# The first weight tile of two up projections in three products of 256 columns

## The chip, the cores and the metric

The kernel runs on one core of a Trainium2 chip. The metric is the device time of one execution in microseconds (us); the number that counts is the median of several executions. TensorE (PE in the profile) multiplies; it has a queue of its own for the loads of its stationary operand (PEld). VectorE (DVE), ScalarE (ACT) and GpSimd (POOL) do the rest, and SyncE (SP) issues the weight transfers.

## The reference: what is computed

One decoder layer on 256 tokens of width 2048 in float32: a norm, a combined input projection, attention in eight heads beside a pooling mixer, an output projection into the residual stream, and then a gated MLP of inner width 5632 with a short convolution over time:

```python
def conv_ffn(h, w_up, conv_w, conv_b, w_down):
    u = h @ w_up
    ...
    for i in range(CONV_WIDTH):
        y = y + conv_w[i] * u_pad[:, i:i + S]
    gate, val = jnp.split(y, 2, axis=-1)
    return (jax.nn.silu(gate) * val) @ w_down

...
    x = x + conv_ffn(rms_norm(x, ffn_norm_g[l]), w_up[l], conv_w[l], conv_b[l], w_down[l])
```

The change lies in `h @ w_up`.

## The kernel before

**High and low parts.** Every float32 operand is split into a rounded part and a remainder: `wh` and `wl` of the weights, index 0 and 1 of the third axis of the activations. A product in float32 is then the sum of three: high by high, high by low, low by high. The rounded copy of a weight chunk is made on ACT (`high`, L150), its remainder on DVE (`low`, L156).

**Chunks.** All weights come as a row of chunks of 128 x 2048, loaded by SP into four `raw` buffers in turn, and each chunk is used in two halves, the steps `u = 2 * c` and `u = 2 * c + 1`. The steps stand in one list, and the loop at the end of `layer` runs through it, so that the order of the products on TensorE is the order of that list.

**Up projections.** A block of 256 output features takes four steps (`feat_block`). Its accumulator `ps_feat` is a pair of PSUM banks from the pool tag `acc`, one bank for each `m`, 512 columns wide: the left 256 columns for the high part of the activations (`S` is 256), the right 256 for everything that is to be added to it. `feat_half` calls `feat_mm` for each of the two banks, and `feat_mm` goes over four weight tiles of 128 x 128. For each it issues two products: `wh` against high and low part side by side, 512 columns (L235), and `wl` against the high part, 256 columns, added to the right half (L237). A weight tile is thus a pair of products, 512 and 256 columns, each with a load of its own of the stationary operand, which here is the weights. The activations are `xh` in the input projection, `cat` in the output projection and `x2h` in the MLP.

**The other forms.** The token-major input projections (`tok_half`, L228; `val_half`, L209 and L218) and the down projection (`product`, L822, called by `seven_products` and `eight_products`) keep the activations stationary and move the weights, in products of 512 columns throughout. The pooling mixer (`feat_sum`, L244) takes three products of 256 columns for each weight tile: `wh` by the high part, `wh` by the low part, `wl` by the high part. Attention (L456, L492, L494) has products of 128 and 256 columns.

**The MLP in thirds.** The inner width is done in three parts (`THIRDS`) of 8, 8 and 6 blocks of 256: the up projections of a part for gate and value, 16, 16 and 12 blocks of 32 weight tiles, and then its down projection into 2048 columns. So there are two places where an up projection follows a down projection: chunk 97, step 194, and chunk 145, step 290. The first third's up projection, from step 98 on, follows the output projection, which is of the same form as itself. Before the down projection's last accumulators are free again, DVE has to add them to the residual (`done`, L900).

Of the kernel before, what the change touches and what calls it, by code (L numbers as in the profile page):

```python
# [31 lines left out]
S = 256  # L32
# [11 lines left out]
HALF = CH // 2  # L44
AHEAD = 5
FROM = 52
RAWS = 4

C_FFN, C_PS, C_QG, C_KG, C_CW, C_CB = 0, 16, 24, 25, 26, 26 + 3 * 2 * NF
# [33 lines left out]
def layer(ctx: ExitStack, tc: tile.TileContext, xT, wts, par, rel_d, ident_d, icnt_d, out):  # L83
    nc = tc.nc
# [15 lines left out]
    def small(name):  # L100
        return sm.tile([P, 512], F32, name=name, tag="small")
# [9 lines left out]
    def load(c, lo=0, n=CH, queue=None):  # L111

        if c not in raws:
            raws[c] = wpool.tile([P, CH], F32, name="raw", tag="raw", bufs=RAWS)
        s = slice(lo, lo + n)
# [24 lines left out]
    def split(c):  # L140
        split_piece(c, 0, CH)
        release(c)
# [3 lines left out]
    def high(c):  # L146

        wparts[c] = w, = (high_tile(c),)
        for lo, n in PIECES.get(kinds[c], ((0, CH),)):
            nc.scalar.activation(w[:, lo:lo + n], raws[c][:, lo:lo + n], AF.Copy)  # L150

    def low(c):

        wh, wl, r = *wparts[c], low_tile(c), raws[c]
        for lo, n in PIECES.get(kinds[c], ((0, CH),)):
            nc.vector.tensor_tensor(wl[:, lo:lo + n], r[:, lo:lo + n], wh[:, lo:lo + n].bitcast(F32), op=OP.subtract)  # L156
        wparts[c] = wh, wl
        if kinds[c] == "seven":
            wparts[c] += right_sums(r)
        release(c)  # L160
# [22 lines left out]
    def half(u):  # L183

        parts = wparts[u // 2] if u % 2 == 0 else wparts.pop(u // 2)
        return tuple(w[:, (u % 2) * HALF:(u % 2 + 1) * HALF] for w in parts)

    def release(c):

        raws.pop(c)  # L190
        c += RAWS
        if c < KT // 2:
# [39 lines left out]
    def feat_mm(ps, wh, wl, act, ks, first, last):  # L232

        for n, (ws, k) in enumerate(ks):
            nc.tensor.matmul(ps, wh[:, ws], act[:, k, :, :],  # L235
                             start=(first and n == 0), stop=False, skip_group_check=True)
            nc.tensor.matmul(ps[:, S:], wl[:, ws], act[:, k, 0, :], start=False,  # L237
                             stop=(last and n == len(ks) - 1), skip_group_check=True)

# [7 lines left out]
    def feat_half(u, act, k0, ps, first, last, mm=feat_mm):  # L247
        wh, wl = half(u)
        for m in range(2):
            mm(ps[m], wh, wl, act,  # L250
               [(slice(k * 256 + m * P, k * 256 + (m + 1) * P), k0 + k) for k in range(4)],
               first, last)


    xh = keep.tile([P, KT, 2, S], F32R, name="xh", tag="h")
# [29 lines left out]
    ps = small("ps_start")  # L285
# [291 lines left out]
    def feat_block(act, ks, post, final=False):  # L577
        box, runs = {}, []
        for i, k0 in enumerate(ks):
            def run(u, i=i, k0=k0):  # L580
                if i == 0:
                    box["acc"] = None if final else acc("ps_feat")
                    box["ps"] = [small("ps_feat")[:, :S] if final else box["acc"][:, m, :] for m in range(2)]
                feat_half(u, act(), k0, box["ps"], i == 0, i == len(ks) - 1, feat_sum if final else feat_mm)
                if i == len(ks) - 1:
                    post(box["ps"] if final else box["acc"])
            runs.append([run])
        return runs
# [46 lines left out]
    for b in range(2):  # L635
# [6 lines left out]
        for j in range(4):  # L642
            h = 4 * b + j
            u, ul, uo = ((32, 35, 40), (40, 44, 48), (48, 52, 55), (55, 59, 63))[h // 2]
# [286 lines left out]
    n = len(steps)  # L931
    assert n == 2 * wts.shape[0], (n, wts.shape)
    for u in range(n):
# [4 lines left out]
        elif u >= 4 and u % 2 == 0:  # L938
            c, now[0] = u // 2 + 2, u
            if c < FROM:  # L940
                split(c)
            if c >= FROM - 1 and c + 1 < wts.shape[0]:
                high(c + 1)
            if FROM <= c < wts.shape[0]:
                splits.append(lambda c=c: low(c))
# [83 lines left out]
```

## Time and profile before

| | us |
|---|---|
| median of 3 executions | 1010.86 |
| lowest, highest | 1009.64, 1010.89 |
| the profiled execution's own time | 1010.22 |
| its span in the trace | 1008.5 |
| mean granted clock of TensorE in it | 0.999 |

A row of a group of instructions reads: line, engine, operation, output and inputs by the program's names, tile sizes, count, then the busy time of the group, the mean duration of one in ns and the idle time ahead of it. A row of the timeline begins with the start and the duration in us. Products overlap in the trace: the next begins while the one before still has its end to write, so a duration is longer than the distance from one start to the next. Busy time counts each moment once. The distance between starts is the time that a product costs in a stream.

### The profile page before, as it was taken

How to read it: one execution, taken by the hardware profiler on the slowest of the kernel's cores; microseconds unless marked ns; L12 is line 12 of the kernel's file. 1: busy time of each engine (PE TensorE's matmuls, PEld its weight loads, DVE VectorE, ACT ScalarE, POOL GpSimd, SP SyncE). 2: the span in 40 equal slices, each digit the busy share in tenths (PEclk: the TensorE clock that was granted, in tenths of full speed). 3: DMA queues.
4: the chain of work that ended last, by engine and by line, in shares of the span. 5: the costliest groups of instructions: out<-in, count | busy, mean ns of one | idle time of the engine just before them, and what ended most of it. 6: DMA issues, size and time to landing. Idle time of an engine off the chain costs nothing.

```text
span 1008.5 us, 13232 instructions
## 1 busy us (share of the span) xinstructions
PE 1002.6 (99%) x5304; PEld 860.8 (85%) x5304; DVE 802.1 (80%) x943; ACT 529.4 (52%) x560; POOL 61.3 (6%) x119
## 2 busy tenths in 40 slices
PE   9999999999999999999999999999999999999998
PEld 8888888888888888888888888888888888888886
DVE  6776859857679878789996777778899867877996
ACT  6554545555556655556453545455564444555641
POOL 0302232200003300000000000000000000000000
PEclk9999999999999999999999999999999999999999
DMA  9958785665558855554556455554554665555361
GB/s 349 316 209 280 253 260 194 212 251 198 218 178 266 301 187 203 202 175 169 207 209 251 167 173 203 182 194 168 183 211 153 245 209 172 204 174 202 127 232 58
DMA packets 36156, 210.34 MB, mean 209 GB/s; under 512 B 5288, under 2 KB 7720, under 8 KB 13184
## 3 DMA queue, kind: packets, MB, share of 16 engines
q1 hardware_dynamic: 31408, 197.58, 55.7%
q0 software_dynamic: 4688, 11.94, 4.2%
q8 instruction: 41, 0.67, 0.3%
q14 instruction: 19, 0.16, 0.0%
HBM read 201.23 MB, written 8.26 MB: 208 GB/s over the span
## 4 chain that ended last, share of the span: by engine, by line
PE 91%; issue 4%; DMA 3%; DVE 1%; POOL 1%; SPq 0%; ACT 0%; POOLq 0%; DVEq 0%
PE ps_feat L235 41%; PE ps_down L822 23%; PE ps_feat L237 20%; PE ps_val L218 4%; PE ps_tok L228 2%; DMA qT<-q1d 1%; DMA eT<-e3d 1%; DMA q0d<-q0x 1%; PE ps_pool L244 1%; DMA eT<-e0d 1%; DMA raw<-in_wts 0%; DVE wl L125 0%; POOL qT L435 0%; DMA e0d<-e0x 0%; PE ps_s L456 0%
## 5 line engine op out<-in xcount | busy, mean ns | idle before, releaser
L235 PE MATMUL ps_feat<-x2h,wh 128*128 128x512 f32 x1408 | 490.8, 394 | 0.0
L237 PE MATMUL ps_feat<-x2h,wl 128*128 128x256 f32 x1408 | 391.3, 278 | 0.0
L235 PEld LDWEIGHTS ps_feat<-x2h,wh 128*128 128x128 f32 x1408 | 263.7, 187 | 63.2
L156 DVE TENSOR_TENSOR wl<-raw,wh 128x2048 fp32r<-128x2048 f32 (+2 forms) x145 | 286.1, 1990 | 3.3 <-issue 3.3
L237 PEld LDWEIGHTS ps_feat<-x2h,wl 128*128 128x128 f32 x1408 | 264.3, 188 | 0.1
L150 ACT ACTIVATE wh<-raw 128x2048 fp32r<-128x2048 f32 (+2 forms) x145 | 241.3, 1676 | 40.9 <-PE ps_down L822 30.8
L822 PE MATMUL ps_down<-wh,hid 128*128 128x512 f32 x512 | 163.2, 389 | 0.0
L125 DVE TENSOR_TENSOR wl<-raw,wh 128x2048 fp32r<-128x2048 f32 (+3 forms) x60 | 119.6, 2000 | 49.7 <-ACT wh L124 41.2
L505 DVE TENSOR_TENSOR fs<-ps_feat,fs 128x512 f32<-128x512 f32 x52 | 35.9, 691 | 107.6 <-ACT fs L504 107.6
L822 PEld LDWEIGHTS ps_down<-wh,hid 128*128 128x128 f32 x512 | 96.1, 188 | 19.9
L124 ACT ACTIVATE wh<-raw 128x2048 fp32r<-128x2048 f32 (+3 forms) x60 | 99.9, 1681 | 10.9 <-DMA raw<-in_wts 7.7
L822 PE MATMUL ps_down<-wl,hid 128*128 128x512 f32 x256 | 99.6, 389 | 0.0
L235 PE MATMUL ps_feat<-cat,wh 128*128 128x512 f32 x256 | 87.3, 389 | 0.0
L504 ACT ACTIVATE fs<-ps_feat 128x512 f32<-128x512 f32 x52 | 31.1, 597 | 94.0 <-PE ps_feat L237 92.1
L228 PE MATMUL ps_tok<-wh,xh 128*128 128x512 f32 x256 | 80.1, 391 | 0.0
L237 PE MATMUL ps_feat<-cat,wl 128*128 128x256 f32 x256 | 70.7, 276 | 0.0
L178 ACT ACTIVATE th<-raw 128x1024 fp32r<-128x1024 f32 x32 | 34.0, 1063 | 50.9 <-DVE raw L167 45.7
L235 PEld LDWEIGHTS ps_feat<-cat,wh 128*128 128x128 f32 x256 | 48.1, 188 | 10.0
L228 PEld LDWEIGHTS ps_tok<-wh,xh 128*128 128x128 f32 x256 | 48.1, 188 | 10.0
L822 PEld LDWEIGHTS ps_down<-wl,hid 128*128 128x128 f32 x256 | 48.0, 188 | 9.9
L797 ACT ACTIVATE hid<-y 128x512 fp32r<-128x512 f32 x22 | 13.9, 633 | 76.8 <-DVE y L796 76.8
L228 PE MATMUL ps_tok<-wl,xh 128*128 128x512 f32 x128 | 49.8, 389 | 0.0
(194 smaller groups left out, 1075.7 us busy)
## 6 DMA issues: line engine op xcount, KB each, us to landing
raw<-in_wts SPq DMA_DIRECT2D x178, 1024.0 KB, 4.8
raw<-in_wts SPq DMA_DIRECT2D x4, 512.0 KB, 7.2
x2d<-x2x POOLq DMA_DIRECT2D x4, 512.0 KB, 6.5
x<-x2d POOLq DMA_DIRECT2D x32, 64.0 KB, 5.8
xboth<-in_xT SPq DMA_DIRECT2D x6, 256.0 KB, 10.0
out<-x SPq DMA_DIRECT2D x3, 512.0 KB, 3.5
x2f<-in_xT SPq DMA_DIRECT2D x1, 1024.0 KB, 8.6
x2f<-in_xT SPq DMA_DIRECT2D x1, 768.0 KB, 6.6
```

The lines of the kernel that those rows point to most:

```text
L124: nc.scalar.activation(wh, w, AF.Copy)
L125: nc.vector.tensor_tensor(wl, w, wh.bitcast(F32), op=OP.subtract)
L150: nc.scalar.activation(w[:, lo:lo + n], raws[c][:, lo:lo + n], AF.Copy)
L156: nc.vector.tensor_tensor(wl[:, lo:lo + n], r[:, lo:lo + n], wh[:, lo:lo + n].bitcast(F32), op=OP.subtract)
L178: nc.scalar.activation(part(t[0]), part(r), AF.Copy)
L218: nc.tensor.matmul(ps[b][:, t, :], xh[:, k, a, ts], w[:, ws], start=False, stop=(k == KT - 1 and n == 2), skip_group_check=True)
L228: nc.tensor.matmul(ps[:, t, :], act[:, k0 + k, a, ts], w[:, ws], start=(first and k == 0 and n == 0), stop=(last and k == 1 and n == 2))
L235: nc.tensor.matmul(ps, wh[:, ws], act[:, k, :, :], start=(first and n == 0), stop=False, skip_group_check=True)
L237: nc.tensor.matmul(ps[:, S:], wl[:, ws], act[:, k, 0, :], start=False, stop=(last and n == len(ks) - 1), skip_group_check=True)
L504: nc.scalar.activation(dst, ps[:, :, S:], AF.Copy)
L505: nc.vector.tensor_tensor(dst, ps[:, :, :S], dst, op=OP.add)
L822: nc.tensor.matmul(ps, a, w, start=(first and n == 0), stop=(last and n == 2), skip_group_check=True)
```

## The change

The constant `AFTER_DOWN` names the two chunks. In their first half, for the first bank (`m == 0`) and the first of the four weight tiles, the product of 512 columns is made as two of 256: one for the high part of the activations into the left half of the bank, one for the low part into the right half. The first of them carries the start flag. The third product, `wl` by the high part, is as before. All else is as before: 2 of the 896 weight tiles of those two up projections are touched.

```diff
+AFTER_DOWN = (97, 145)
...
     def feat_mm(ps, wh, wl, act, ks, first, last):
 
         for n, (ws, k) in enumerate(ks):
-            nc.tensor.matmul(ps, wh[:, ws], act[:, k, :, :],
-                             start=(first and n == 0), stop=False, skip_group_check=True)
+            if first == "apart" and n == 0:
+                for a in range(2):
+                    nc.tensor.matmul(ps[:, a * S:(a + 1) * S], wh[:, ws], act[:, k, a, :],
+                                     start=(a == 0), stop=False, skip_group_check=True)
+            else:
+                nc.tensor.matmul(ps, wh[:, ws], act[:, k, :, :],
+                                 start=(bool(first) and n == 0), stop=False, skip_group_check=True)
             nc.tensor.matmul(ps[:, S:], wl[:, ws], act[:, k, 0, :], start=False,
                              stop=(last and n == len(ks) - 1), skip_group_check=True)
...
             mm(ps[m], wh, wl, act,
                [(slice(k * 256 + m * P, k * 256 + (m + 1) * P), k0 + k) for k in range(4)],
-               first, last)
+               "apart" if first and m == 0 and u // 2 in AFTER_DOWN else first, last)
```

TensorE's queue at the first place, step 194, where the down projection of the first third ends. `ps_down` are its accumulators, `hid` its stationary activations; the numbers tell buffers apart. Before:

```order
L822 MATMUL ps_down_4292<-wl_4460,hid_2672 128x512
L822 MATMUL ps_down_4292<-wh_4428,hid_2672 128x512
L235 MATMUL ps_feat_4563<-x2h_1931,wh_4458 128x512 [waits DVE_49,Activation_49]
L237 MATMUL ps_feat_4563<-x2h_1931,wl_4497 128x256
L235 MATMUL ps_feat_4563<-x2h_1931,wh_4458 128x512
L237 MATMUL ps_feat_4563<-x2h_1931,wl_4497 128x256
```

And with the change (the products' lines are now L828, L238 for the two halves, L241 for 512 columns and L243 for `wl`):

```order
L828 MATMUL ps_down_4292<-wl_4460,hid_2672 128x512
L828 MATMUL ps_down_4292<-wh_4428,hid_2672 128x512
L238 MATMUL ps_feat_4563<-x2h_1931,wh_4458 128x256 [waits DVE_49,Activation_49]
L238 MATMUL ps_feat_4563<-x2h_1931,wh_4458 128x256
L243 MATMUL ps_feat_4563<-x2h_1931,wl_4497 128x256
L241 MATMUL ps_feat_4563<-x2h_1931,wh_4458 128x512
L243 MATMUL ps_feat_4563<-x2h_1931,wl_4497 128x256
```

One row has become two, with the wait on the first of them; nothing else has moved. The second place, step 290, where the down projection of the second third ends, on the same engine, before:

```order
L822 MATMUL ps_down_6329<-wh_6465,hid_4733 128x512
L235 MATMUL ps_feat_6600<-x2h_1931,wh_6495 128x512 [waits DVE_49,Activation_49]
L237 MATMUL ps_feat_6600<-x2h_1931,wl_6534 128x256
L235 MATMUL ps_feat_6600<-x2h_1931,wh_6495 128x512
L237 MATMUL ps_feat_6600<-x2h_1931,wl_6534 128x256
```

And with the change:

```order
L828 MATMUL ps_down_6330<-wh_6466,hid_4734 128x512
L238 MATMUL ps_feat_6601<-x2h_1931,wh_6496 128x256 [waits DVE_49,Activation_49]
L238 MATMUL ps_feat_6601<-x2h_1931,wh_6496 128x256
L243 MATMUL ps_feat_6601<-x2h_1931,wl_6535 128x256
L241 MATMUL ps_feat_6601<-x2h_1931,wh_6496 128x512
L243 MATMUL ps_feat_6601<-x2h_1931,wl_6535 128x256
```

Here too one row is two, and the rest stands as it was (the buffers' numbers are one higher, for the product that came in earlier). On DVE, ACT, POOL and SP the instructions and their order are the same in both kernels.

## The prediction

> **What bounds the kernel now.** I read the page first, its busy times and the chain that ended last:
>
> ```profile
> span 1008.5 us, 13232 instructions
> PE 1002.6 (99%) x5304; PEld 860.8 (85%) x5304; DVE 802.1 (80%) x943; ACT 529.4 (52%) x560; POOL 61.3 (6%) x119
> ...
> PE ps_feat L235 41%; PE ps_down L822 23%; PE ps_feat L237 20%; PE ps_val L218 4%; PE ps_tok L228 2%; DMA qT<-q1d 1%; DMA eT<-e3d 1%; DMA q0d<-q0x 1%; PE ps_pool L244 1%; DMA eT<-e0d 1%; DMA raw<-in_wts 0%; DVE wl L125 0%; POOL qT L435 0%; DMA e0d<-e0x 0%; PE ps_s L456 0%
> ```
>
> TensorE has work all the time, and the chain is made of its products. So there is hardly a wait to remove, and the time changes only if products themselves follow each other at another distance. That is the second thing to read. The busy times by stage, for two stretches of 160 us, the first within the up projection of the first third, the second within that of the second third, and one within that of the last third (columns: PE, PEld, DVE, ACT, POOL, clock, DMA share, GB/s):
>
> ```profile
> 285.00:445.00 160.00, 160.00 (x943) 141.54 (x942) 132.54 (x164) 90.84 (x97) 20.66 (x38) 1.00 0.67 222
> 542.20:702.20 160.00, 160.00 (x908) 138.20 (x907) 117.82 (x137) 83.20 (x85) 0.00 (x0) 1.00 0.55 191
> 806.10:941.70 135.60, 135.60 (x770) 117.16 (x769) 101.59 (x118) 70.47 (x73) 0.00 (x0) 1.00 0.54 187
> ```
>
> In the same 160 us, TensorE is busy throughout in both stretches and its granted clock is 1.00 in both, yet it makes 943 products in the first and 908 in the second. The two up projections are the same code with the same tile sizes. The groups by shape, over the whole of each up projection, give the size of it:
>
> ```profile
> L235 PE MATMUL ps_feat<-x2h,wh 128*128 128x512 f32 x512 | 174.1, 389 | 0.0
> ...
> L235 PE MATMUL ps_feat<-x2h,wh 128*128 128x512 f32 x512 | 180.9, 397 | 0.0
> ...
> L235 PE MATMUL ps_feat<-x2h,wh 128*128 128x512 f32 x384 | 135.7, 397 | 0.0
> ```
>
> A product of 512 columns lasts past the start of the next of its kind, so the busy time of this group is the stage without a gap, and divided by the count it is the distance from one pair (512 and 256 columns) to the next: 174.1 / 512 = 340.0 ns in the first third, 180.9 / 512 = 353.3 ns in the second, 135.7 / 384 = 353.4 ns in the last. I call these the short and the long pace. The difference is 13.3 ns a pair.
>
> **What separates the two.** Since clock, code and shapes are equal, I looked at how each stretch of pairs begins. The timeline of TensorE at the place of the change, out of the down projection:
>
> ```profile
> 541.88 0.39 PE L822 MATMUL ps_down<-wh,hid 128*128 128x512 f32 x1
> 542.11 0.39 PE L235 MATMUL ps_feat<-x2h,wh 128*128 128x512 f32 x1
> 542.34 0.28 PE L237 MATMUL ps_feat<-x2h,wl 128*128 128x256 f32 x1
> 542.46 0.40 PE L235 MATMUL ps_feat<-x2h,wh 128*128 128x512 f32 x1
> 542.69 0.28 PE L237 MATMUL ps_feat<-x2h,wl 128*128 128x256 f32 x1
> 542.81 0.40 PE L235 MATMUL ps_feat<-x2h,wh 128*128 128x512 f32 x1
> ...
> 805.98 0.39 PE L235 MATMUL ps_feat<-x2h,wh 128*128 128x512 f32 x1
> 806.21 0.28 PE L237 MATMUL ps_feat<-x2h,wl 128*128 128x256 f32 x1
> 806.33 0.40 PE L235 MATMUL ps_feat<-x2h,wh 128*128 128x512 f32 x1
> ...
> 806.68 0.40 PE L235 MATMUL ps_feat<-x2h,wh 128*128 128x512 f32 x1
> ```
>
> No product waits here: the first pair follows the last product of the down projection after 0.23 us, as those follow each other. The pairs are at the long pace from the first on (542.11, 542.46, 542.81), and both places look the same to the hundredth. A third stretch comes directly out of products of 512 columns, in the input projection behind L228, and it has the long duration of 397 ns as well:
>
> ```profile
> L235 PE MATMUL ps_feat<-xh,wh 128*128 128x512 f32 x8 | 2.9, 397 | 0.0
> ```
>
> Those 8 pairs end where attention's small products cut in. Behind these, and behind the pooling mixer's products of 256 columns, the groups are others:
>
> ```profile
> L235 PE MATMUL ps_feat<-xh,wh 128*128 128x512 f32 x52 | 17.7, 389 | 0.0
> ...
> L235 PE MATMUL ps_feat<-xh,wh 128*128 128x512 f32 x61 | 20.8, 389 | 0.0
> ...
> L235 PE MATMUL ps_feat<-cat,wh 128*128 128x512 f32 x230 | 78.3, 389 | 0.0
> ```
>
> The first two of these groups stand behind attention's products, from 148.9 and from 170.5 us on, and have 17.7 / 52 = 340 and 20.8 / 61 = 341 ns a pair; the third stands behind the mixer's products, from 207.1 us on, with 78.3 / 230 = 340. How TensorE comes into the last of them:
>
> ```profile
> 206.01 0.28 PE L244 MATMUL ps_pool<-cat,wl 128*128 128x256 f32 x1
> 206.13 0.39 PE L235 MATMUL ps_feat<-cat,wh 128*128 128x512 f32 x1
> ...
> 206.48 0.40 PE L235 MATMUL ps_feat<-cat,wh 128*128 128x512 f32 x1
> ...
> 206.84 0.39 PE L235 MATMUL ps_feat<-cat,wh 128*128 128x512 f32 x1
> ...
> 207.18 0.39 PE L235 MATMUL ps_feat<-cat,wh 128*128 128x512 f32 x1
> ```
>
> The pairs from 206.13 on are 0.35, 0.36 and 0.34 us apart: they begin at about the long pace and find the short one within three pairs. That stretch, once in, runs to the end of the first third's up projection without leaving it. So there are two steady paces; a stretch of pairs falls into one of them in its first microsecond and stays there for hundreds of pairs, and which one depends on what TensorE did just before. In this trace all entries from a product of 512 columns into a pair go to the long pace (three), all entries by way of shorter products to the short one: the three of the quoted groups, and two shorter stretches between them that do the same.
>
> **The change part by part.** It replaces the first pair at both places by three products of 256 columns, in the order `wh`, `wh`, `wl` in which the mixer makes its own.
>
> *The products themselves.* The chain of work has the mixer's 24 products in a row as one piece, start and length in us:
>
> ```profile
> 197.90 2.82 PE ps_pool L244 x24
> ```
>
> A product of 256 columns in a row of its like costs 2.82 / 24 = 0.118 us. Three of them are 0.354 us in place of the first pair's 0.35 (542.11 to 542.46): nothing that the rows resolve, at most 0.01 us at each of the two places. Their additional load of the stationary operand is in that distance already, since each of the mixer's products has its own. The wait on ACT and DVE moves to the first of the three and nothing was waited for there; behind it the queue is as before. Bounds: nothing below, and 0.24 us above, if each of the two additional products came on top with its whole 0.118 us.
>
> *The pace behind them.* This is the term that matters and that the trace doesn't show for this sequence: no stretch in it comes out of 512 columns by way of only three of 256. The nearest rows bound it: 353.3 ns a pair if nothing changes, 340.0 ns if the alternation locks into the short pace. I take the short pace, because the last three products ahead of the pair at 206.13 are the same three in the same order with the same weight layout, and that entry goes to the short pace in three pairs. Then the second third gains 180.9 − 174.1 = 6.8 us, and the last 135.7 − 384 x 0.3400 = 5.1 us. Together 11.9 us. Each entry costs some of it: the three pairs from 206.13 to 207.18 took 1.05 us, 0.03 over 3 x 0.340, so with the three products 0.04 us a place, 0.1 for both.
>
> *What could take it back.* A quicker TensorE asks for weights sooner. The first third shows that the rest keeps up: at 340 ns it had DVE at 132.54 of 160 us with more beside it than the later thirds have (the residual's turn on POOL), ACT at 90.84 and the DMA engines at 0.67, and PE 160.00 of 160. So no new bound is late next. The down projections keep their own pace.
>
> The sum: 1010.22 for the profiled execution, − 11.9 + 0.1 = 998.4 us. That execution is 0.64 below the median of the runs, 1010.86, from which it would be 999.1; I predict 998.8.
>
> **A rule that speaks against it.** The trace's rows above say that one and the same pair of products costs 340.0 or 353.3 ns at the same granted clock. The Trainium skill, in "TensorE: Matmul & The Clock Gate", section "Back-to-back issue gap", gives the distance of a warm product as its columns over 2.4 GHz and about 2.5 ns, with no memory of what came before. By that rule a pair of 512 and 256 columns is an estimated 325 ns everywhere, the change adds two products and no columns, an estimated 5 ns in all, and the time stays. The trace disagrees with it twice, by the level and by having two of them, so I give this outcome the chance of the second rival only.
>
> **The rivals.**
>
> 1. *One place only.* The first sequence locks into the short pace and the other doesn't, or the pace is lost on the way. For it: the trace shows single entries, not why. Against it: the entries at 542.11 and 805.98 are alike in every start, and no long stretch changes its pace. With the second third alone 1010.22 − 6.8 = 1003.4, with the last alone 1005.1; 0.6 more from the median.
> 2. *Nothing.* Three products of 256 columns are too few, or what decides was set in the down projection; the pairs go on at 353. For it: at the long pace too each 512 follows a 256, and that doesn't free it; and the mixer's entry followed 24 short products, not three. The price is that of the two additional products, under 0.24 us: 1010.2, from the median 1010.9.
> 3. *A worse pace, slower.* The alternation locks beyond 353 ns. For it: pairs of 0.36 us are seen while a stretch settles (206.48 to 206.84). Against it: no stretch stays there. If all 896 pairs ran at 0.36 us, it would be 896 x 6.7 ns = 6.0 us more, 1016.2; it decides the sign measurably from 2.0 / 896 = 2.2 ns over the long pace.
>
> **How the numbers follow.** Both places at the short pace 0.70, one place 0.07, nothing 0.20, a worse pace 0.03. A measurement of this kernel tells a change of about 0.2%, or 2 us, from none. So faster 0.77, same 0.21, slower 0.02 (a third of the worst case stays within 2 us). The forecast's own range is 997.6 to 1000.2: 998.4 and 999.1 with the spread of the three runs. It holds 0.70, so the range has to reach to the case of no change, up to 1011.2.
>
> **What would show each step.** In the changed kernel's trace the groups of L241, 512 columns, should have about 174 us for 511 pairs in the second third and 130.5 for 383 in the last, mean durations of 389 and not 397 ns, and TensorE's products in 160 us behind the first place should be some 943 and not 908. The timeline should show three starts about 0.12 us apart, then two or three pairs of 0.35 and from there 0.34. The last third should start 6.8 us sooner. If the pairs behind the three products stay 0.35 apart, the step on the entry is wrong and the time stays near 1010.5; if they reach 0.34 but TensorE then shows idle time behind DVE or a weight transfer, the step on the cover is wrong.

## The result, and the profile after

The changed kernel takes 998.22 us, median of 4 runs (997.55 to 999.07), against 1010.8 before: a ratio of 0.9879, with a 95% interval of 0.9867 to 0.989. The profiled execution took 999.07 us, its span 997.3.

The page's first lines for the changed kernel, to be read beside those of before: TensorE is busy for 99% as it was. It has two products more and is busy 11.9 us less, in a span that is 11.2 us shorter.

```profile
span 997.3 us, 13236 instructions
## 1 busy us (share of the span) xinstructions
PE 990.7 (99%) x5306; PEld 856.8 (86%) x5306; DVE 802.1 (80%) x943; ACT 528.9 (53%) x560; POOL 61.4 (6%) x119
```

The busy times of the changed kernel by stretch, the same columns and, for the first two, the same stretches as before:

```profile
285.00:445.00 160.00, 160.00 (x943) 141.91 (x942) 131.87 (x164) 90.25 (x95) 20.73 (x38) 1.00 0.67 222
542.20:702.20 160.00, 160.00 (x943) 141.68 (x942) 123.65 (x144) 84.71 (x88) 0.00 (x0) 1.00 0.57 195
799.50:930.00 130.50, 130.50 (x769) 115.42 (x768) 101.14 (x117) 69.70 (x72) 0.00 (x0) 1.00 0.56 195
```

160 us of the second third now hold 943 products, as many as in the first third, where they held 908. The granted clock is 1.00 throughout, so the clock is no part of it. The groups of the changed kernel's wide products by stage: the second third, the last third, and a stretch of the input projection from 148.9 to 166.2 us:

```profile
L241 PE MATMUL ps_feat<-x2h,wh 128*128 128x512 f32 x511 | 173.8, 389 | 0.0
...
L241 PE MATMUL ps_feat<-x2h,wh 128*128 128x512 f32 x383 | 130.3, 389 | 0.0
...
L241 PE MATMUL ps_feat<-xh,wh 128*128 128x512 f32 x51 | 18.1, 397 | 0.0
```

173.8 / 511 and 130.3 / 383 are both 340 ns a pair: the short pace, at both places. The third row is one that the prediction did not expect. The same stretch in the same 17.3 us had 52 pairs at a mean duration of 389 ns before, and has 51 at 397 now: the long pace, in a part of the program that the change does not touch.

How TensorE of the changed kernel comes out of the down projection, start and duration in us:

```profile
542.55 0.39 PE L828 MATMUL ps_down<-wh,hid 128*128 128x512 f32 x1
542.78 0.40 PE L238 MATMUL ps_feat<-x2h,wh 128*128 128x256 f32 x2
543.01 0.28 PE L243 MATMUL ps_feat<-x2h,wl 128*128 128x256 f32 x1
543.13 0.39 PE L241 MATMUL ps_feat<-x2h,wh 128*128 128x512 f32 x1
...
543.48 0.40 PE L241 MATMUL ps_feat<-x2h,wh 128*128 128x512 f32 x1
...
543.84 0.39 PE L241 MATMUL ps_feat<-x2h,wh 128*128 128x512 f32 x1
...
799.88 0.40 PE L238 MATMUL ps_feat<-x2h,wh 128*128 128x256 f32 x2
```

Three products in 0.35 us, pairs 0.35 and 0.36 apart, then the short pace.

The difference of the two profiled executions closes from these starts. The first place is reached at 542.78 in place of 542.11, 0.67 us later; that is the stretch at the long pace above, some 55 pairs x 13.3 ns = 0.7. So the last third starts 6.1 us sooner, at 799.88, and not the 6.8 of the gain alone. From the first place to the second it takes 257.10 in place of 263.87 us, 6.77 less; from the second to the end of the span 197.4 in place of 202.5, 5.1 less. 0.67 − 6.77 − 5.1 = − 11.2, and the spans differ by 1008.5 − 997.3 = 11.2.

### The profile page after: what moved, and what is told of

It reads as the page before. It is cut to its first block, busy times and chain, and to the rows that moved or that the text cites. A ratio compares the mean times of both kernels' runs of the same rounds, so it can differ in the third digit from the quotient of the medians.

```text
span 997.3 us, 13236 instructions
## 1 busy us (share of the span) xinstructions
PE 990.7 (99%) x5306; PEld 856.8 (86%) x5306; DVE 802.1 (80%) x943; ACT 528.9 (53%) x560; POOL 61.4 (6%) x119
## 4 chain that ended last, share of the span: by engine, by line
PE 91%; issue 4%; DMA 3%; DVE 1%; POOL 1%; SPq 0%; ACT 0%; POOLq 0%; DVEq 0%
PE ps_feat L241 41%; PE ps_down L828 23%; PE ps_feat L243 20%; PE ps_val L219 4%; PE ps_tok L229 2%; DMA qT<-q1d 1%; DMA eT<-e3d 1%; DMA q0d<-q0x 1%; PE ps_pool L250 1%; DMA eT<-e0d 1%; DMA raw<-in_wts 0%; DVE wl L126 0%; POOL qT L441 0%; DMA e0d<-e0x 0%; PE ps_s L462 0%
## 5 line engine op out<-in xcount | busy, mean ns | idle before, releaser
L241 PE MATMUL ps_feat<-x2h,wh 128*128 128x512 f32 x1406 | 478.2, 389 | 0.0
L243 PE MATMUL ps_feat<-x2h,wl 128*128 128x256 f32 x1408 | 388.6, 276 | 0.0
L241 PEld LDWEIGHTS ps_feat<-x2h,wh 128*128 128x128 f32 x1406 | 263.9, 188 | 54.6
L243 PEld LDWEIGHTS ps_feat<-x2h,wl 128*128 128x128 f32 x1408 | 264.3, 188 | 0.0
L828 PE MATMUL ps_down<-wh,hid 128*128 128x512 f32 x512 | 163.3, 389 | 0.0
L828 PEld LDWEIGHTS ps_down<-wh,hid 128*128 128x128 f32 x512 | 96.1, 188 | 20.0
L828 PE MATMUL ps_down<-wl,hid 128*128 128x512 f32 x256 | 99.6, 389 | 0.0
L241 PE MATMUL ps_feat<-cat,wh 128*128 128x512 f32 x256 | 87.3, 389 | 0.0
L243 PE MATMUL ps_feat<-cat,wl 128*128 128x256 f32 x256 | 70.7, 276 | 0.0
L828 PEld LDWEIGHTS ps_down<-wl,hid 128*128 128x128 f32 x256 | 48.1, 188 | 9.9
L241 PEld LDWEIGHTS ps_feat<-cat,wh 128*128 128x128 f32 x256 | 48.1, 188 | 9.8
```

What stands on the lines that cost most here:

```text
L241: nc.tensor.matmul(ps, wh[:, ws], act[:, k, :, :], start=(bool(first) and n == 0), stop=False, skip_group_check=True)
L828: nc.tensor.matmul(ps, a, w, start=(first and n == 0), stop=(last and n == 2), skip_group_check=True)
```

## The experiments

What was to be told apart: does each entry set the pace of its own stretch; does it take three products, halves, or anything short; is it the entry alone or can a stretch be freed later; does a row of 512-column products lead to the long pace by itself; and what makes two paces out of one sequence of products.

### One place alone

```diff
-AFTER_DOWN = (97, 145)
+AFTER_DOWN = (97,)
```

> The first product apart at chunk 97 only. Theory (each stretch of pairs keeps the pace into which its own entry led it): 512 pairs of the second third at 340 ns, 384 of the last at 353, so 6.7 us less than before, about 1004.1. Rival (the first place resets something for the rest of the program): the last third at 340 too, about 998.3.

Measured 1004.12 us (3 runs), ratio 0.9938 with 0.9916 to 0.9961. Its second third has 173.1 us for 509 pairs, the short pace. The group of its last third:

```profile
L241 PE MATMUL ps_feat<-x2h,wh 128*128 128x512 f32 x384 | 135.7, 397 | 0.0
```

The last third is back at 135.7 us, to the tenth what it was. Each entry sets its own stretch, and the two gains add up.

### The same three products half way

```diff
-AFTER_DOWN = (97, 145)
+AFTER_DOWN = (113, 157)
```

> The same three products, not at the entry but half way through the two up projections (chunks 113 and 157, 256 and 192 pairs after their entries). If the pace is fixed at the entry alone: no pair faster, about 1010.8. If any such trio throws the pairs out of the long pace: 256 and 192 pairs 13.3 ns shorter, 6.0 us less, about 1004.8.

1010.76 us (8 runs), ratio 1.0003 with 0.9992 to 1.0014: nothing. The groups of that kernel's second third, ahead of the three products and behind them:

```profile
L241 PE MATMUL ps_feat<-x2h,wh 128*128 128x512 f32 x256 | 90.5, 397 | 0.0
...
L241 PE MATMUL ps_feat<-x2h,wh 128*128 128x512 f32 x255 | 90.1, 397 | 0.0
```

90.5 / 256 and 90.1 / 255 are both 353 to 354 ns, and the last third is the same on both sides (67.9 / 192 and 67.5 / 191). The very three products that work at the entry do not free a stretch that is in the long pace. What they are does not decide alone, then; it also counts where they stand, behind the down projection or among the pairs.

### One short product, uneven parts, and one wide product

Three other ways to come in. The first reorders each weight tile from chunk 97 on, the 256 columns of `wl` ahead of the 512 of `wh`:

```diff
+        if now[0] >= SWAP:
+            for n, (ws, k) in enumerate(ks):
+                nc.tensor.matmul(ps[:, S:], wl[:, ws], act[:, k, 0, :],
+                                 start=(first and n == 0), stop=False, skip_group_check=True)
+                nc.tensor.matmul(ps, wh[:, ws], act[:, k, :, :], start=False,
+                                 stop=(last and n == len(ks) - 1), skip_group_check=True)
+            return
```

> From chunk 97 on each weight tile makes its 256 columns (wl) first and its 512 (wh) second: no product more, the same alternation, but the entry out of the down projection is by one product of 256. If any shorter product between 512 and the pairs is enough: 340 ns in both, about 998.3. If it takes a row of several short ones: 353 ns, about 1010.8.

998.43 us (2 runs), ratio 0.9879 with 0.985 to 0.9908. Its entry has no settling at all:

```profile
541.93 0.39 PE L830 MATMUL ps_down<-wh,hid 128*128 128x512 f32 x1
542.16 0.28 PE L237 MATMUL ps_feat<-x2h,wl 128*128 128x256 f32 x1
542.27 0.39 PE L239 MATMUL ps_feat<-x2h,wh 128*128 128x512 f32 x1
542.50 0.28 PE L237 MATMUL ps_feat<-x2h,wl 128*128 128x256 f32 x1
542.62 0.39 PE L239 MATMUL ps_feat<-x2h,wh 128*128 128x512 f32 x1
542.84 0.28 PE L237 MATMUL ps_feat<-x2h,wl 128*128 128x256 f32 x1
```

The products of 256 columns stand at 542.16, 542.50 and 542.84: 0.34 us from the first pair on. So the same products in another order within the tile are enough; not one need be added. The other order holds here in every tile from chunk 97 on, not at the two entries only.

The second cuts the first product of the changed kernel at 384 columns at the one place and at 128 at the other:

```diff
-                for a in range(2):
-                    nc.tensor.matmul(ps[:, a * S:(a + 1) * S], wh[:, ws], act[:, k, a, :],
-                                     start=(a == 0), stop=False, skip_group_check=True)
+                cut, x = CUT[now[0] // 2], act[:, k, :, :].rearrange("p a t -> p (a t)")
+                for lo, hi in ((0, cut), (cut, 2 * S)):
+                    nc.tensor.matmul(ps[:, lo:hi], wh[:, ws], x[:, lo:hi],
+                                     start=(lo == 0), stop=False, skip_group_check=True)
```

> The first product cut unevenly: 384 and 128 columns at chunk 97, 128 and 384 at chunk 145. If any shorter product between the down projection and the pairs is enough: 340 ns in both, about 998.3. If it takes the equal halves, whose distances the pairs are made of: 353 ns in one or both, 1003.6 to 1010.6.

998.81 us (2 runs), ratio 0.9882 with 0.9863 to 0.9902. Both places are at the short pace, with 173.8 us for 511 pairs and 130.3 for 383. Equal halves are not needed.

The third makes one `wl` product wider in place of a `wh` product shorter, at the first entry and, in the last third, half way:

```diff
+            if first and ws.start == 0 and now[0] // 2 in WIDE:
+                nc.tensor.matmul(ps, wl[:, ws], act[:, k, :, :], start=False, stop=False, skip_group_check=True)
+                continue
```

> One wl product made 512 wide (wl by the low part is added too): that of the first weight tile at chunk 97, the entry, and that of one tile half way through the last third, at chunk 157. Each costs 0.1 us. If what matters is that the first pair out of the down projection meets the 227 ns beat of its products, one product more at that width delays the pair but not the beat, and the second third stays at 353 ns; and half way nothing changes either: about 1010.8. If any irregular product does it: 340 ns in the second third and in the last half of the last, 6.8 and 2.6 us less, about 1001.2.

1001.12 us (2 runs), ratio 0.9905 with 0.9885 to 0.9925, as the second expectation had it. The second third has 173.8 us for 511 pairs, as in the changed kernel. The groups of the last third, ahead of the wide product and behind it:

```profile
L236 PE MATMUL ps_feat<-x2h,wh 128*128 128x512 f32 x192 | 67.9, 397 | 0.0
...
L236 PE MATMUL ps_feat<-x2h,wh 128*128 128x512 f32 x190 | 64.7, 389 | 0.0
```

67.9 / 192 is 354 ns and 64.7 / 190 is 341. Here a stretch is freed half way, at the very weight tile of chunk 157 where three short products did nothing, and at the entry a product that is not shorter but wider works as well. So short products are not what it takes. My expectation that one more product at the old width would leave the beat as it was is refuted. That "any irregular product does it" is not so either, as the three short ones half way show.

### A row of wide products ahead of the first third

The 16 `wl` products of chunk 49 are made 512 columns wide, so that the first third's pairs too come out of a row of 32 such products:

```diff
+            if now[0] == WIDE:
+                nc.tensor.matmul(ps, wl[:, ws], act[:, k, :, :], start=False,
+                                 stop=(last and n == len(ks) - 1), skip_group_check=True)
+                continue
```

> Chunk 49, the first of the first third's up projection, makes its 16 wl products 512 columns wide (wl by the low part is then added too, which the kernel leaves out), so that 32 products of 512 stand in a row ahead of pairs that ran at the short pace. Their own cost is 16 x 113 ns = 1.8 us. Theory (a run of 512 columns followed by a pair gives the long pace, whatever the operands): the other 496 pairs of that third go to 353 ns, 6.6 us more, about 1019.2 in all. Rival (it is the down projection's operands, or its place): they stay at 340 ns, about 1012.6.

1012.52 us (8 runs), ratio 1.002 with 1.0009 to 1.0031: the price of the wide products and no more. The first product of the row, its end, and the group of the 496 pairs behind it:

```profile
285.38 0.39 PE L236 MATMUL ps_feat<-x2h,wh 128*128 128x512 f32 x1
...
292.77 0.40 PE L236 MATMUL ps_feat<-x2h,wh 128*128 128x512 f32 x1
293.01 0.28 PE L242 MATMUL ps_feat<-x2h,wl 128*128 128x256 f32 x1
293.13 0.39 PE L236 MATMUL ps_feat<-x2h,wh 128*128 128x512 f32 x1
...
L236 PE MATMUL ps_feat<-x2h,wh 128*128 128x512 f32 x496 | 168.7, 389 | 0.0
```

168.7 / 496 is 340 ns. A pair directly behind a row of 512 columns can come out at the short pace; the theory loses this one. The row itself does not run like the down projection's. From 285.38 to 293.01 its 32 wide products and the first of the pair behind them take 7.63 us, or 231 ns each; the down projection of before, from its chain of work, start and length in us:

```profile
459.29 82.98 PE ps_down L822 x366
```

82.98 / 366 is 227 ns. So it doesn't leave TensorE at the same beat, and the run does not say what the down projection's own operands do.

### All tiles in the other order

The order of the run with one short product, `wl` first, in all projections of this form (its condition on `now` is left out).

> The 256 columns (wl) first in every weight tile of every projection of this form, from the input projection on. If one short product at an entry is enough everywhere: both MLP thirds at 340 ns as in the run with this order from chunk 97 on, and the 7 pairs behind L228 and the stretch behind attention that fell to 353 ns in some runs at 340 too: 0.1 to 0.8 us below the changed kernel, about 997.7. If an entry out of small products is open either way: 998.3, with one of the input projection's stretches at 353 ns.

999.1 us (4 runs), ratio 0.9883 with 0.9867 to 0.99; nothing won over the changed kernel. In its profile all stretches are at the short pace but one of the output projection, at 192.8 us, behind attention, where before had 389 ns:

```profile
L238 PE MATMUL ps_feat<-cat,wh 128*128 128x512 f32 x14 | 5.0, 397 | 0.0
```

The input projection's stretches are at 340 ns, as the first expectation had it, yet the time is not lower for it; neither expectation had the output projection's. So this order is no safeguard: either pace can follow attention in it, too.

### Other addresses for the low part

In the last kind of run the products, their order and their entries are those of before. Only the place of the low weight parts within their buffer is moved, by 16 bytes or more. The constant holds for all chunks of this form, so those of the input projection, the mixer and the output projection move with those of the up projections, of which alone the expectations speak:

```diff
-WOFF = ((32, 32), (16, 36))
+WOFF = ((32, 32), (16, 32))
```

> The kernel before, with the low weight parts of the up projections laid 16 bytes lower in their buffer (128 in place of 144 bytes in), nothing else. If the paces come from the reads of the weight load meeting the reads of the moving operand at related addresses: another distance than 340.0 and 353.3 ns in at least one third, so a time off by more than 2 us either way. If they come from the order and number of the products alone: the first third at 340, the others at 353, about 1010.6.

997.83 us (2 runs), ratio 0.9873 with 0.9853 to 0.9892. The entry out of the down projection, and the groups of the second and the last third:

```profile
541.36 0.40 PE L235 MATMUL ps_feat<-x2h,wh 128*128 128x512 f32 x1
...
541.71 0.39 PE L235 MATMUL ps_feat<-x2h,wh 128*128 128x512 f32 x1
...
542.05 0.39 PE L235 MATMUL ps_feat<-x2h,wh 128*128 128x512 f32 x1
...
L235 PE MATMUL ps_feat<-x2h,wh 128*128 128x512 f32 x512 | 174.1, 389 | 0.0
...
L235 PE MATMUL ps_feat<-x2h,wh 128*128 128x512 f32 x384 | 130.6, 389 | 0.0
```

The pair follows directly on the down projection's 512 columns, in the same order as in the kernel before, and the first takes 0.35 us as there; the second already takes 0.34, and the stretch stays there. The input and the output projection are at 340 ns as well, the pairs behind L228 included. So the time is off by 12 us, as the first expectation had it, but not by another distance: the short pace holds everywhere. Two more places, 208 bytes (`(16, 52)`) and 160 bytes (`(16, 40)`) in:

> The kernel before with the low weight parts of the up projections 208 bytes into their buffer (144 before): 64 bytes on, so at the same place within 64 bytes. If the place within 64 bytes decides whether the long pace is met: 340, 353, 353 ns as before, about 1010.5. If any move of the buffer's contents upsets it: 340 ns in a later third as well, 1005.4 or less.

> The kernel before with the low weight parts 160 bytes in: 32 past a multiple of 64, where before has 16 and the aligned run 0. If every place but the aligned one meets the long pace: about 1010.5. If it is the 16 alone: 340 ns in all thirds, about 998.

1010.13 us (8 runs), ratio 0.9997 with 0.9986 to 1.0007, and 1010.38 us (8 runs), ratio 1.0 with 0.999 to 1.001. By the times, both are the kernel before. By the groups they are not; first, second and last third at 208 bytes:

```profile
L235 PE MATMUL ps_feat<-x2h,wh 128*128 128x512 f32 x512 | 177.5, 394 | 0.0
L235 PE MATMUL ps_feat<-x2h,wh 128*128 128x512 f32 x512 | 177.5, 393 | 0.0
L235 PE MATMUL ps_feat<-x2h,wh 128*128 128x512 f32 x384 | 133.2, 393 | 0.0
```

And at 160 bytes, the second third, the others being like it:

```profile
L235 PE MATMUL ps_feat<-x2h,wh 128*128 128x512 f32 x512 | 177.6, 390 | 0.0
```

177.5 / 512 is 347 ns, in all three thirds. At 160 bytes each pair takes 346 or 347 ns; at 208 single distances go from 342 to 353 and make 347 on average. There is one mean pace here, between the two, and the three thirds have it behind different entries: the first third has lost 3.4 us, the later two have won 3.4 and 2.5. The 2.5 us won on balance are largely lost again in the pairs of the input and the output projection, which are at 347 ns too: at 208 bytes, 232 wide products of the output projection take 80.5 us. The expectations named the time and missed this. Both hypotheses about which byte within 64 decides fall: 208 bytes, at the same place within 64 as 144, gives other paces than 144, and 160 gives neither 340 nor 353. The times alone would have passed as "no difference".

Last, the aligned kernel and the changed one side by side, with more runs of the former:

> The aligned kernel (128 bytes in, products as before the change) once more, with more rounds. If it is the better of the two because no stretch of the input projection meets the long pace either: 997.8, some 0.3 to 0.7 us below the changed kernel, with all stretches at 340 ns. If it is the same thing by other means: the same within 0.3 us.

> The changed kernel again beside it. Both theories: 998.2, with the stretch behind attention at 148 us at 340 or at 353 ns, by chance.

998.8 and 998.85 us (4 runs each), ratios 0.9883 (0.9868 to 0.9898) and 0.9884 (0.9867 to 0.99). They are the same. The aligned kernel has all its stretches at 340 ns again, and is still not the better one by anything that these runs can tell; the two kernels get the same gain by different edits. In the changed kernel's profile the stretch behind attention, from 148.9 to 166.2 us, is at the short pace this time:

```profile
L241 PE MATMUL ps_feat<-xh,wh 128*128 128x512 f32 x52 | 17.7, 389 | 0.0
```

The same program, the same instructions, 397 ns in one execution and 389 in another.

## Why the prediction was right, point by point

**The bound.** TensorE's products were the whole time, and nothing was late next: PE stayed at 160.00 of 160 us in the second third at 943 products, with DVE at 123.65. That step held.

**The products themselves.** Three in 0.35 us (542.78 to 543.13) for a pair of 0.35: nothing, as taken.

**The size.** 6.8 and 5.1 us were predicted for the two thirds, and 6.77 and 5.1 are what lies between the starts. The sum for the profiled execution was 998.4; it took 999.07. The 0.67 between is no part of the change. It is the input projection's stretch behind attention, which ran at the long pace in this execution.

**The entry.** The forecast that both places lock into the short pace held, and so did that they go alike and keep it. The reason given for it did not hold as a rule. That entries from a product of 512 columns lead to the long pace, and entries by way of shorter products to the short one, described one trace. Behind attention the same instructions of the same input projection come out at 389 ns in one profile of the changed kernel and at 397 in another; a row of 512 columns led to the short pace; a wider product frees a stretch half way and three short ones don't. Short products are one way of meeting the pairs otherwise, not the cause. So the sum is right in each of its terms, but that these three products would meet the pairs rightly was in part luck: nothing in the trace told them from the same three half way, where they do nothing. The 0.20 for "nothing" was fair for that reason, and not for the one that was given, that three may be too few: in the run with the other order one short product at the entry is enough.

**The rivals.** One place only: built for itself, it gave 1004.12 against 1003.4 for the execution and 1004.0 from the median. Nothing: it did not come at the entry; the same products half way gave it, 1010.76. A worse pace: none beyond 353 ns was seen in a steady stretch in any run, though the steady pace can have other values than the two, 347 ns at other addresses.

**The rule that spoke against it.** A pair at 340.0, 347 or 353.3 ns, with equal columns and a granted clock of 1.00, stands against a distance that follows from the columns alone, as the prediction took it from the Trainium skill's "TensorE: Matmul & The Clock Gate", section "Back-to-back issue gap". That section of the Trainium skill calls its formula the gap of a product by itself, and says that in a stream the loads and the products set the spacing together; the prediction passed over this. The outcome that the formula stood for, no gain, did not come.

**What the cause is, as far as the runs show it.** Moving the low weight parts by 16 bytes, with every product as before, changes the distance of the pairs. These parts are read by the loads of the stationary operand, and the loads run while the product ahead reads its moving operand: in the trace of before, the load for the product at 542.34 starts with the product at 542.11:

```profile
542.11 0.39 PE L235 MATMUL ps_feat<-x2h,wh 128*128 128x512 f32 x1
542.11 0.19 PEld L237 LDWEIGHTS ps_feat<-x2h,wl 128*128 128x128 f32 x1
```

Work of the other engines does not hold a stretch at its pace. By the starts in the trace of before, 104 pairs of the second third run while VectorE, which writes the low parts, does nothing, and 315 while it is busy throughout; each of them takes 353 or 354 ns. In the first third each takes 340, with VectorE idle or busy, and it is likewise with ScalarE in both. Whether the other engines have a part in which pace a stretch falls into, no run shows. Both products of a pair are later in the long pace: from start to start the wide one takes 236 ns and the other 117.5, where the short pace has 227 and 113.

That the two sets of reads get in each other's way, depending on addresses and on where in the stream they meet, and that the alternation settles into whichever meeting repeats itself, fits every run. It was not shown directly: no run has one of the two reads alone. The Trainium skill says in "TensorE: Matmul & The Clock Gate", section "Step-by-step: what each phase is for", that loading the next tile's weights "doesn't steal SBUF read bandwidth from the running matmul". These runs don't agree without more: the low weight parts' address alone moves a pair from 353.3 to 340.0 or 347 ns, though they don't show that it is bandwidth that is short.

Open remain why three short products work at the entry and not half way, why one and the same program can take either pace behind attention, and which addresses go with which paces; four places of the low part were tried, and none of the high part or of the activations.

## What to carry to other kernels

When one and the same sequence of products runs at two distances in one trace, at equal clock and without waits, compare how the stretches begin before looking for an engine to blame, and compare the busy time per product of each stage rather than the sum. Try the order within a tile and the address of the stationary operand first; neither adds a product, and here each was worth as much as the added ones. And read the stages even where the total does not move: here 347 ns everywhere and 340 with 353 gave the same time.

## What the runs showed of the hardware that had not been expected

- A stream of alternating 512 and 256 columns has more than one steady distance: 340.0, 353.3 and, at other addresses of the stationary operand, 347 ns a pair. It keeps one for hundreds of pairs.
- The same instructions can fall into either in different executions: the stretch behind attention had 397 ns a wide product in one profile of the changed kernel and 389 in another. That is 0.7 us a run, within the spread of the runs.
- 16 bytes in the place of the low weight parts were worth 12 us in this kernel, without an instruction changed.
